# Completing each inverse to a whole token tile in the delta rule of a hybrid decoder layer

## The chip, the cores and the metric

The kernel runs on one core of a Trainium2 chip. The time is the device time of one launch in microseconds. Engines are named as the profile names them: PE (TensorE's products), PEld (its weight loads), DVE (VectorE), ACT (ScalarE), POOL (GpSimd), SP (SyncE, which issues most DMAs).

## The reference

One decoder layer on 256 tokens of width 2048: a normed input, one wide projection, two token mixers beside each other, gates, an output projection, a norm and a residual. All in float32. The change concerns the first mixer, the gated delta rule, of 8 heads of width 128, which is defined on chunks of 64 tokens:

```python
kb = k * beta[..., None]; vb = v * beta[..., None]
L = jnp.where(strict, jnp.einsum('bhnid,bhnjd->bhnij', kb, k) * decay, 0.0)
T = triangular_solve(L + eye, eye, left_side=True, lower=True)
u = jnp.einsum('bhnij,bhnje->bhnie', T, vb)
w = jnp.einsum('bhnij,bhnjd->bhnid', T, kb * jnp.exp(g)[..., None])
...
def step(state, inp):          # over the chunks
    v_new = u_i - jnp.einsum('bhcd,bhde->bhce', w_i, state)
    o = einsum(qg_i, state) + einsum(a_i, v_new)
    state = state * gl_i[..., None, None] + jnp.einsum('bhcd,bhce->bhde', kd_i, v_new)
```

With the decays carried along, this is one lower triangular system per head over the tokens: the new values of a stretch of tokens are its inverse triangle times (values less what earlier stretches contribute). It gives the same values whether it is cut in four stretches of 64 or in two of 128.

## The kernel before

Tokens lie in NT = 2 tiles of P = 128. The projections are the bulk of the work: `proj_t` and `proj_n` read weights in blocks of 1 MB over SP's queue, split each into a high and a low part (ACT and DVE, lines 225 and 226), and multiply in float32r. After every few products they call `tick()`. A tick counts half a unit, and lets the queues go on: each queue holds Python generators that issue some work and yield how many units to wait. So all the rest of the layer is issued between projection products, at places set by the yields: `SV_WAIT = 1` is two ticks, `L_WAIT = 5` is ten. PE takes its products in exactly the order in which they are issued (`mm` on line 147, `tr` on line 150, both pinned).

The delta rule is in the queue `gq`, in this order: `score_pair` for each pair of heads, `inverse`, `solve`.

`score_pair` writes `sl(h)`, the decayed products of keys and of queries, per head and token tile, and stores the four 64x64 triangles of each head to `l_d` in DRAM.

`inverse` inverts all 32 triangles (4 chunks, 8 heads) at once on DVE, 63 steps of two operations with `tv` and `tw`, issued at line 657 and 664. It stores the result to `t_d` (line 667) and loads it transposed into the tile `tt` (line 673), all on POOL's queue, and yields `L_WAIT`. `inv[0]` holds, for token tile t and head h, the transposed inverse of the first 64 tokens on partitions 0 to 63 (`lo_`) and that of the second 64 on partitions 64 to 127 (`hi_`).

`solve` waits until the values are there (`vq`), then goes through seven calls of `step(t, which)`, each followed by a yield of `SV_WAIT`. Every call makes 8 products (one per head) into two PSUM tiles named `sv`, and empties these into the values `gvt`:

- `which` 0: the first 64 tokens' inverse times their values (ACT copies, line 902)
- `which` 1: the triangle's lower left block times these, taken off the second 64 tokens' values (DVE, line 904)
- `which` 2: the second 64 tokens' inverse times their values (ACT, line 906)
- `which` 3, between the two token tiles: the first tile's contribution to the second, 128x128 (DVE, line 908)

Then `normed` makes the outputs (`so`), norms and gates them into `oz`, branch weights are fetched, and, after all attention heads have passed their transposes (`attended`), `turned_outputs` transposes the outputs (`ot`). The attention of the other mixer (`ms`, `pp`, `po`) runs in queues of its own between the same projections. PSUM has four `aux` banks for all this small work and four for the projections.

Of the kernel before, what the change touches and what calls it, by code (L numbers as in the profile page):

```python
# [8 lines left out]
F32 = mybir.dt.float32  # L9
# [3 lines left out]
ALU = mybir.AluOpType  # L13
AX = mybir.AxisListType

P = 128
# [16 lines left out]
SV_WAIT = 1  # L33
# [41 lines left out]
def hybrid_layer(  # L75
# [15 lines left out]
    nc = tc.nc  # L91
    B, S, D = x.shape
    NT = S // P
    KT = D // P
    H = a_log.shape[1]
# [17 lines left out]
    big = ctx.enter_context(tc.tile_pool(name="big", bufs=1))  # L113
# [10 lines left out]
    def acc_tile(name):  # L124
        return acc.tile([P, 512], F32, tag="acc", name=name)

    def aux_tile(name):
        return aux.tile([P, 512], F32, tag="aux", name=name)
# [17 lines left out]
    def mm(*args, **kwargs):  # L146
        return pin(nc.tensor.matmul(*args, **kwargs))  # L147

    def tr(*args):
        return pin(nc.tensor.transpose(*args))  # L150
# [26 lines left out]
    ident = cst.tile([P, P], F32, name="ident")  # L177
# [59 lines left out]
    def turn(c):  # L237

        pts = []
        for k in range(4 * c, 4 * c + 4):  # L240
            if k % 2 == 0:
                pt = aux_tile(f"hTp_{k}")
            pts.append((k, pt[:, k % 2 * S : (k % 2 + 1) * S]))
            for t in range(NT):
                tr(pts[-1][1][:, t * P : (t + 1) * P], xs[t][:, k * P : (k + 1) * P], ident)
        return pts
# [48 lines left out]
    pts = turn(0)  # L295
# [185 lines left out]
    gsl, gvt = [], []  # L481
# [5 lines left out]
    def sl(h):  # L487
        return gsl[h // HG][:, h % HG, :]

    def vt(t, h):  # L490
        return gvt[h // HG][:, t, h % HG, :]
# [9 lines left out]
    t_d = dram.tile([4, H, 64, 64], F32, name="t_d")  # L501
# [107 lines left out]
    def queries(p):  # L609
        h = 2 * p  # L610
        pq = proj_t(CQ + h * P, f"q{h}")
        qTs = [halves(pq[m], f"q{h + m}") for m in range(2)]
        for m in range(2):
            conv_silu(qTs[m], h + m)
        gq.add(score_pair(h, kTs[p], qTs))
        if p == H // 2 - 1:
            gq.add(inverse())
            gq.add(solve())


    inv = []

    def inverse():
        lc = big.tile([P, 64, 64], F32, tag="u1", name="lc")
        tv = big.tile([P, 16, 64], F32, tag="tv", name="tv")
        tw = big.tile([P, 16, 64], F32, tag="tw", name="tw")

        nc.gpsimd.memset(tv, 1.0)
        for g in range(4):
            nc.gpsimd.affine_select(  # L630
                out=tv[32 * g : 32 * g + 32],
                in_=tv[32 * g : 32 * g + 32],
                compare_op=ALU.is_equal,
                fill=0.0,
                base=g,
                pattern=[[4, 16], [-1, 64]],
                channel_multiplier=0,
            )

        rows = [slice(16 * r, 16 * r + 16) for r in range(4)]  # L640
        yield 0.5
        for js in rows:
            nc.gpsimd.dma_start(lc[0:32, js], l_d.rearrange("b h j i -> (b h) j i")[:, js])

        def copy(r, g):
            pin(nc.scalar.copy(lc[32 * g : 32 * g + 32, rows[r]], lc[0:32, rows[r]]))

        yield LC_WAIT
        for g in range(1, 4):
            copy(0, g)  # L650
            yield 0.5
        for j in range(63):
            if j < 48 and j % 16 in (4, 7, 10):
                copy(j // 16 + 1, (j % 16 - 1) // 3)
            n, r = j // 4 + 1, 63 - j
            pin(
                nc.vector.tensor_tensor(
                    tw[:, :n, :r],
                    lc[:, j : j + 1, j + 1 :].to_broadcast([P, n, r]),
                    tv[:, :n, j : j + 1].to_broadcast([P, n, r]),  # L660
                    op=ALU.mult,
                )
            )
            pin(nc.vector.tensor_tensor(tv[:, :n, j + 1 :], tv[:, :n, j + 1 :], tw[:, :n, :r], op=ALU.subtract))
            yield INV[after[0] > 0]
        for g in range(4):
            nc.gpsimd.dma_start(
                t_d.rearrange("b h (c g) i -> g (b h) c i", g=4)[g], tv[32 * g : 32 * g + 32]
            )
        inv.append(big.tile([P, NT, H, 64], F32, tag="tt", name="tt"))  # L670
        for p_ in range(2):
            for t in range(NT):
                nc.gpsimd.dma_start(
                    inv[0][p_ * 64 : p_ * 64 + 64, t, :, :], t_d[2 * t + p_].rearrange("h c i -> c h i")
                )
        yield L_WAIT


    def v_tok(h, vT):
        yield V_WAIT if h % 2 == 0 else 0.5  # L680
        while sc_left[0]:
            yield 1
        pv = aux_tile(f"vt_{h}")
        for t in range(NT):
            tr(pv[:, t * P : (t + 1) * P], vT[:, t * P : (t + 1) * P], ident)
        nc.vector.tensor_tensor(
            gvt[h // HG][:, :, h % HG, :],
            pv[:, : 2 * P].rearrange("p (t e) -> p t e", t=NT),
            sk[:, :, h : h + 1].to_broadcast([P, NT, P]),
            op=ALU.mult,  # L690
        )
# [182 lines left out]
    def solve():  # L874
        oT = big.tile([P, H, 2 * S], F32R, tag="u1", name="oaT")
        oaT[0] = oT
        lo_, hi_ = slice(0, 64), slice(64, 128)

        def step(t, which):
            for g in range(2):  # L880
                ps = aux_tile(f"sv_{t}_{which}_{g}")
                p3 = ps.rearrange("p (h e) -> p h e", e=P)
                for hh in range(4):
                    h = g * 4 + hh
                    o_ = slice(hh * P, (hh + 1) * P)
                    if which == 0:
                        mm(ps[lo_, o_], inv[0][lo_, t, h, :], vt(t, h)[lo_], start=True, stop=True)
                    elif which == 1:
                        mm(
                            ps[hi_, o_],  # L890
                            sl(h)[lo_, t * 4 * P + 64 : t * 4 * P + 128],
                            vt(t, h)[lo_],
                            start=True,
                            stop=True,
                        )
                    elif which == 2:
                        mm(ps[hi_, o_], inv[0][hi_, t, h, :], vt(t, h)[hi_], start=True, stop=True)
                    else:
                        mm(ps[:, o_], sl(h)[:, P : 2 * P], vt(0, h), start=True, stop=True)
                v_ = gvt[g][:, t]  # L900
                if which == 0:
                    nc.scalar.copy(v_[lo_], p3[lo_])
                elif which == 1:
                    nc.vector.tensor_tensor(v_[hi_], v_[hi_], p3[hi_], op=ALU.subtract)
                elif which == 2:
                    nc.scalar.copy(v_[hi_], p3[hi_])
                else:
                    nc.vector.tensor_tensor(gvt[g][:, 1], gvt[g][:, 1], p3, op=ALU.subtract)

# [83 lines left out]

        while vq.items or v_left[0]:
            yield 1
        for t in range(NT):
            for which in range(3):
                step(t, which)
                yield SV_WAIT
            if t == 0:  # L1000
                step(0, 3)
                yield SV_WAIT
        ozs = [big.tile([P, 2, HG, P], F32, tag=tg, name=f"oz_{t}") for t, tg in enumerate(("tv", "tw"))]
        for t in range(NT):
            yield from normed(t, ozs[t])
# [106 lines left out]
    for blk in ORDER:  # L1112
        n, c = blk[:2].rstrip("0123456789"), int(blk[-1])
# [123 lines left out]
    for tg, n in (("g0", 4), ("ga", 4), ("u1", 4)):  # L1237
        tl = big.tile([P, n, 2, 512], F32R, tag=tg, name=f"keep_{tg}")
# [22 lines left out]
    c = 3  # L1261
    pts = [acc_tile(f"a_y{c}_{t}") for t in range(NT)]
# [43 lines left out]
```

## Time and profile before

| | us |
|---|---|
| three runs | 778.04, 778.52, 779.99 |
| median | 778.52 |
| the profiled execution | 777.05 |
| its span in the trace | 775.4 |
| first and last product of the solve start (`sv`) | 365.1 and 397.6 |

The profile is of one execution. Its page gives the busy time of each engine, the chain of work that ended last, and the costliest groups of instructions; a row of a timeline gives the start and duration in us, then engine, line, operation, what is written and read, and shapes. Products of f32 by f32 appear as two records each, their f32 transposes as one. "[idle before <- releaser]" is how long the engine stood idle and what ended it. Records of PE overlap: the next one starts before the end of the one before, so distances between starts count.

### The profile page before, as it was taken

Reading aid. Unit: us, or ns where it says so; the run is one execution under the profiler, and the core shown is the slowest. Engines: PE = TensorE matmul, PEld = TensorE weight load, DVE = VectorE, ACT = ScalarE, POOL = GpSimd, SP = SyncE. Lnnn points to the kernel's source line nnn. Section 1 sums busy time; section 2 is a strip of 40 time slices with the busy share of each in tenths; the row PEclk is TensorE's granted clock in tenths of the full one; section 3 lists DMA queues with packets and bytes.
Section 4 is the critical chain, followed back from the end, with each engine's and each line's share of the span. In section 5 each row is a group of like instructions: output and inputs, shape, how many; then the busy total and the mean of one; then the engine's idle time right before and its main releaser. Section 6 shows DMA issues by size and latency. Waiting matters only on the chain.

```text
span 775.4 us, 10348 instructions
## 1 busy us (share of the span) xinstructions
PE 763.5 (98%) x3923; PEld 650.2 (84%) x3923; DVE 565.2 (73%) x914; ACT 436.1 (56%) x654; POOL 33.5 (4%) x61
## 2 busy tenths in 40 slices
PE   8999999999999999999999999999999999999995
PEld 7898988899888888888889888788888888888884
DVE  5777669885878898775547886686658776888853
ACT  5676666657655664454447475654455544556731
POOL 3000001112000000002001000000000000000000
PEclk9999999999999999999999999999999999999999
DMA  8576675457655556668336556657644956375912
GB/s 302 173 238 214 188 213 170 136 166 220 202 179 202 177 188 196 198 180 217 109 97 217 178 173 216 242 205 251 212 163 152 386 172 212 111 286 193 333 54 109
DMA packets 93656, 151.87 MB, mean 196 GB/s; under 512 B 3237, under 2 KB 46886, under 8 KB 93094
## 3 DMA queue, kind: packets, MB, share of 16 engines
q1 hardware_dynamic: 88902, 134.42, 53.4%
q0 software_dynamic: 4128, 15.74, 6.0%
q10 hardware_dynamic: 576, 1.05, 0.4%
q8 instruction: 31, 0.51, 0.3%
q14 instruction: 19, 0.16, 0.1%
HBM read 148.04 MB, written 3.15 MB: 195 GB/s over the span
## 4 chain that ended last, share of the span: by engine, by line
PE 95%; ACT 2%; DVE 2%; DMA 1%; SPq 0%; issue 0%; DVEq 0%
PE a_gb L147 11%; PE a_y L147 11%; PE a_ga L147 11%; PE a_zg L147 6%; PE a_mq L147 6%; PE a_v L147 6%; PE a_mk L147 6%; PE a_ub L147 6%; PE a_zm L147 6%; PE a_mv L147 5%; PE a_k L147 5%; PE a_ua L147 5%; PE a_q L147 4%; PE sv L147 2%; PE s L147 1%; DMA x<-in_x_dram 1%
## 5 line engine op out<-in xcount | busy, mean ns | idle before, releaser
L147 PE MATMUL a_ga<-hi_ga,hT 128*128 128x512 f32 x256 | 81.9, 393 | 0.0
L147 PE MATMUL a_gb<-hi_gb,hT 128*128 128x512 f32 x256 | 80.2, 390 | 0.0
L226 DVE TENSOR_TENSOR lo_gb<-raw_gb,hi_gb 128x1024 fp32r<-128x1024 f32 x32 | 38.9, 1223 | 25.1 <-ACT hi_gb L225 24.9
L147 PEld LDWEIGHTS a_gb<-hi_gb,hT 128*128 128x128 f32 x256 | 48.0, 188 | 10.6
L147 PEld LDWEIGHTS a_ga<-hi_ga,hT 128*128 128x128 f32 x256 | 48.1, 188 | 10.1
L225 ACT CAST hi_gb<-raw_gb 128x1024 fp32r<-128x1024 f32 x32 | 33.3, 1051 | 35.6 <-PE a_gb L147 26.5
L225 ACT CAST hi_ga<-raw_ga 128x1024 fp32r<-128x1024 f32 x32 | 33.7, 1055 | 34.0 <-PE a_ga L147 16.2
L226 DVE TENSOR_TENSOR lo_ga<-raw_ga,hi_ga 128x1024 fp32r<-128x1024 f32 x32 | 39.0, 1222 | 18.5 <-ACT hi_ga L225 18.3
L147 PE MATMUL a_ga<-lo_ga,hT 128*128 128x512 f32 x128 | 50.0, 391 | 0.1
L147 PE MATMUL a_gb<-lo_gb,hT 128*128 128x512 f32 x128 | 50.0, 391 | 0.0
L147 PE MATMUL a_zg<-hi_zg,hT 128*128 128x348 f32 (+1 forms) x192 | 47.0, 322 | 0.0
L147 PE MATMUL a_mq<-hT,hi_mq 128*128 128x512 f32 x128 | 46.8, 407 | 0.0
L147 PE MATMUL a_mk<-hT,hi_mk 128*128 128x512 f32 x128 | 46.1, 402 | 0.0
L147 PE MATMUL a_y<-hi_y,mT 128*128 128x512 f32 x144 | 46.1, 392 | 0.0
L147 PE MATMUL a_q<-hT,hi_q 128*128 128x512 f32 x128 | 46.0, 399 | 0.0
L147 PE MATMUL a_v<-hT,hi_v 128*128 128x512 f32 x128 | 45.3, 399 | 0.0
L147 PE MATMUL a_ub<-hi_ub,obT 128*128 128x512 f32 x128 | 41.3, 395 | 0.0
L147 PE MATMUL a_k<-hT,hi_k 128*128 128x512 f32 x128 | 40.6, 399 | 0.5 <-ACT hi_k L278 0.5
L147 PE MATMUL a_zm<-hi_zm,hT 128*128 128x512 f32 x128 | 40.5, 392 | 0.0
L147 PE MATMUL a_mv<-hi_mv,hT 128*128 128x512 f32 x128 | 40.1, 391 | 0.0
L147 PE MATMUL a_v<-hT,lo_v 128*128 128x256 f32 x128 | 35.9, 281 | 0.0
L147 PE MATMUL a_q<-hT,lo_q 128*128 128x256 f32 x128 | 35.9, 281 | 0.0
(377 smaller groups left out, 1972.8 us busy)
## 6 DMA issues: line engine op xcount, KB each, us to landing
raw_ga<-in_w_in_dram SPq DMA_DIRECT2D x16, 1024.0 KB, 5.1
raw_gb<-in_w_in_dram SPq DMA_DIRECT2D x16, 1024.0 KB, 5.7
raw_y<-in_w_out_dram SPq DMA_DIRECT2D x15, 1024.0 KB, 5.9
raw_q<-in_w_in_dram SPq DMA_DIRECT2D x8, 1024.0 KB, 5.6
raw_mv<-in_w_in_dram SPq DMA_DIRECT2D x8, 1024.0 KB, 5.1
raw_v<-in_w_in_dram SPq DMA_DIRECT2D x8, 1024.0 KB, 5.7
raw_zm<-in_w_in_dram SPq DMA_DIRECT2D x8, 1024.0 KB, 5.0
raw_mq<-in_w_in_dram SPq DMA_DIRECT2D x8, 1024.0 KB, 5.8
```

The costliest lines, as they stand in the source:

```text
L147: return pin(nc.tensor.matmul(*args, **kwargs))
L225: nc.scalar.copy(hi, raw)
L226: nc.vector.tensor_tensor(lo, raw, hi.bitcast(F32), op=ALU.subtract)
```

## The change

`inverse` no longer ends with the loads. The two token tiles get a tile each, `inv[t]` of 128 partitions x 8 heads x 128, in the tags `tt` and `tw`. POOL clears the quarter that stays zero and loads the two transposed 64x64 inverses onto the diagonal. After `L_WAIT` three groups of small products follow, each over both token tiles and all heads, each followed by `SV_WAIT`: `tl` transposes the first inverse back, `ltl` multiplies the lower left block of the triangle by it, `tlt` multiplies that by the second inverse; with its sign turned it is the fourth quarter. `tmp`, in the tag `tv`, holds the two results between. In `solve` each token tile then needs one step with its 128x128 inverse, and the step between the tiles stays: three calls of `step` in place of seven.

```diff
--- before.py
+++ after.py
@@ -667,14 +667,41 @@
             nc.gpsimd.dma_start(
                 t_d.rearrange("b h (c g) i -> g (b h) c i", g=4)[g], tv[32 * g : 32 * g + 32]
             )
-        inv.append(big.tile([P, NT, H, 64], F32, tag="tt", name="tt"))
-        for p_ in range(2):
-            for t in range(NT):
-                nc.gpsimd.dma_start(
-                    inv[0][p_ * 64 : p_ * 64 + 64, t, :, :], t_d[2 * t + p_].rearrange("h c i -> c h i")
-                )
+
+        for t, tag in enumerate(("tt", "tw")):
+            tl = big.tile([P, H, P], F32, tag=tag, name=f"inv_{t}")
+            inv.append(tl)
+            nc.gpsimd.memset(tl[64:P, :, 0:64], 0.0)
+            for p_ in range(2):
+                ps = slice(p_ * 64, p_ * 64 + 64)
+                nc.gpsimd.dma_start(tl[ps, :, ps], t_d[2 * t + p_].rearrange("h c i -> c h i"))
         yield L_WAIT
 
+        lo_, hi_ = slice(0, 64), slice(64, 128)
+        tmp = big.tile([P, NT, H, 64], F32, tag="tv", name="tmp")
+
+        def blocks(name):
+            pts = [aux_tile(f"{name}_{t}") for t in range(NT)]
+            return [pt.rearrange("p (h c) -> p h c", h=H) for pt in pts]
+
+        pb = blocks("tl")
+        for t in range(NT):
+            for h in range(H):
+                tr(pb[t][lo_, h, :], inv[t][lo_, h, 0:64], ident[lo_, lo_])
+            nc.scalar.copy(tmp[lo_, t], pb[t][lo_])
+        yield SV_WAIT
+        pb = blocks("ltl")
+        for t in range(NT):
+            for h in range(H):
+                mm(pb[t][hi_, h, :], sl(h)[lo_, t * 4 * P + 64 : t * 4 * P + 128], tmp[lo_, t, h], start=True, stop=True)
+            nc.scalar.copy(tmp[hi_, t], pb[t][hi_])
+        yield SV_WAIT
+        pb = blocks("tlt")
+        for t in range(NT):
+            for h in range(H):
+                mm(pb[t][lo_, h, :], tmp[hi_, t, h], inv[t][hi_, h, 64:128], start=True, stop=True)
+            nc.vector.tensor_scalar_mul(inv[t][lo_, :, 64:128], pb[t][lo_], -1.0)
+        yield SV_WAIT
 
     def v_tok(h, vT):
         yield V_WAIT if h % 2 == 0 else 0.5
@@ -874,8 +901,6 @@
     def solve():
         oT = big.tile([P, H, 2 * S], F32R, tag="u1", name="oaT")
         oaT[0] = oT
-        lo_, hi_ = slice(0, 64), slice(64, 128)
-
         def step(t, which):
             for g in range(2):
                 ps = aux_tile(f"sv_{t}_{which}_{g}")
@@ -883,27 +908,10 @@
                 for hh in range(4):
                     h = g * 4 + hh
                     o_ = slice(hh * P, (hh + 1) * P)
-                    if which == 0:
-                        mm(ps[lo_, o_], inv[0][lo_, t, h, :], vt(t, h)[lo_], start=True, stop=True)
-                    elif which == 1:
-                        mm(
-                            ps[hi_, o_],
-                            sl(h)[lo_, t * 4 * P + 64 : t * 4 * P + 128],
-                            vt(t, h)[lo_],
-                            start=True,
-                            stop=True,
-                        )
-                    elif which == 2:
-                        mm(ps[hi_, o_], inv[0][hi_, t, h, :], vt(t, h)[hi_], start=True, stop=True)
-                    else:
-                        mm(ps[:, o_], sl(h)[:, P : 2 * P], vt(0, h), start=True, stop=True)
-                v_ = gvt[g][:, t]
+                    w = inv[t][:, h, :] if which == 0 else sl(h)[:, P : 2 * P]
+                    mm(ps[:, o_], w, vt(0 if which else t, h), start=True, stop=True)
                 if which == 0:
-                    nc.scalar.copy(v_[lo_], p3[lo_])
-                elif which == 1:
-                    nc.vector.tensor_tensor(v_[hi_], v_[hi_], p3[hi_], op=ALU.subtract)
-                elif which == 2:
-                    nc.scalar.copy(v_[hi_], p3[hi_])
+                    nc.scalar.copy(gvt[g][:, t], p3)
                 else:
                     nc.vector.tensor_tensor(gvt[g][:, 1], gvt[g][:, 1], p3, op=ALU.subtract)
 
@@ -993,13 +1001,9 @@
 
         while vq.items or v_left[0]:
             yield 1
-        for t in range(NT):
-            for which in range(3):
-                step(t, which)
-                yield SV_WAIT
-            if t == 0:
-                step(0, 3)
-                yield SV_WAIT
+        for t, which in ((0, 0), (0, 1), (1, 0)):
+            step(t, which)
+            yield SV_WAIT
         ozs = [big.tile([P, 2, HG, P], F32, tag=tg, name=f"oz_{t}") for t, tg in enumerate(("tv", "tw"))]
         for t in range(NT):
             yield from normed(t, ozs[t])
```

## The prediction

> **What bounds the kernel now.** I read the page first: the busy times and the chain that ended last.
>
> ```profile
> span 775.4 us, 10348 instructions
> ...
> PE 763.5 (98%) x3923; PEld 650.2 (84%) x3923; DVE 565.2 (73%) x914; ACT 436.1 (56%) x654; POOL 33.5 (4%) x61
> ...
> PE 95%; ACT 2%; DVE 2%; DMA 1%; SPq 0%; issue 0%; DVEq 0%
> ```
>
> TensorE (PE) is in 95% of the chain. The waits of PE alone confirm it: these four are all it has.
>
> ```profile
> PE hTp L150 <- DMA x<-in_x_dram: 1.5, 2, 0.9
> PE warm L147 <- DVE epst L181: 1.1, 1, 1.1
> PE ms L147 <- DVE y_mk L1084: 0.7, 1, 0.7
> PE a_k L147 <- ACT hi_k L278: 0.5, 1, 0.5
> ```
>
> None of them stands in the solve. So a product taken out of PE's stream shortens the kernel by the time it held the stream, and one put in lengthens it. Work on ACT, DVE and POOL counts only where PE comes to wait for it. Next I asked for the instructions that write or read `sv`, the PSUM tiles of the solve.
>
> ```profile
> L147 PEld LDWEIGHTS sv<-gdn,tt x64: 129/133/133, 365.1 to 397.5; 64*64 64x64 f32 x64
> L147 PE MATMUL sv<-gdn,tt x64: 269/269/320, 365.1 to 397.6; 64*64 64x128 f32 x64
> L147 PEld LDWEIGHTS sv<-gdn x48: 129/133/192, 369.9 to 392.6; 64*64 64x64 f32 x32, 128*128 128x128 f32 x16
> L902 ACT COPY gdn<-sv x4: 579/580/581, 366.2 to 387.5; 64x512 f32<-64x512 f32 x4
> L904 DVE TENSOR_TENSOR gdn<-gdn,sv x4: 691/691/691, 371.1 to 393.1; 64x512 f32<-64x512 f32 x4
> L906 ACT COPY gdn<-sv x4: 581/581/581, 377.6 to 397.9; 64x512 f32<-64x512 f32 x4
> L908 DVE TENSOR_TENSOR gdn<-gdn,sv x2: 680/683/686, 382.2 to 382.9; 128x512 f32<-128x512 f32 x2
> ```
>
> A product of f32 by f32 is two records: the 32 products with the inverse (two half-steps, two token tiles, eight heads) are the x64 of the first row. In all there are 112 records in seven groups of 16: six groups of 64x64 and one of 128x128. A duration in these rows (269 ns) is not what a record holds the stream for, since matmuls are pipelined. For that I read starts in the timeline of PE, around the first 64x64 group and around the 128x128 one.
>
> ```profile
> 364.88 0.28 PE L147 MATMUL a_mq<-hT,lo_mq 128*128 128x256 f32 x1
> 365.09 1.96 PE L147 MATMUL sv<-gdn,tt 64*64 64x128 f32 x16
> 366.98 0.50 PE L147 MATMUL a_mq<-hT,hi_mq 128*128 128x512 f32 x1
> 367.32 0.28 PE L147 MATMUL a_mq<-hT,lo_mq 128*128 128x256 f32 x1
> 367.44 0.39 PE L147 MATMUL a_mq<-hT,hi_mq 128*128 128x512 f32 x1
> 367.67 0.27 PE L147 MATMUL a_mq<-hT,lo_mq 128*128 128x256 f32 x1
> ...
> 380.78 0.27 PE L147 MATMUL a_mq<-hT,lo_mq 128*128 128x256 f32 x1
> 380.89 1.95 PE L147 MATMUL sv<-gdn 128*128 128x128 f32 x16
> 382.60 0.47 PE L147 MATMUL a_mq<-hT,hi_mq 128*128 128x512 f32 x1
> 382.91 0.28 PE L147 MATMUL a_mq<-hT,lo_mq 128*128 128x256 f32 x1
> ```
>
> Undisturbed, a 256-column record is followed after 0.12 us (367.32 to 367.44) and a 512-column one after 0.23 us (367.44 to 367.67): the time goes with the columns. So after the record at 364.88 the next 256-column one was due at 364.88+0.12+0.23 = 365.23; it came at 367.32. **A 64x64 group costs 2.09 us.** The same sum at 380.78 gives 381.13 against 382.91: **the 128x128 group costs 1.78 us.** Its 16 records start 1.71 us apart from what follows (380.89 to 382.60), 0.107 us each. Taking the same for the 64x64 group, 2.09-1.71 = 0.38 us of it lie around the records: it starts 0.21 instead of 0.12 us after its predecessor, and the products behind it start late. The solve as it stands: 6x2.09+1.78 = **14.32 us**. (Three groups are followed by attention products, which share a little of the 0.38; I leave that in on both sides.)
>
> **The change, part by part: PE.** Six 64x64 groups and one of 128x128 go. In come, each between two yields: `tl`, 16 transposes of 64x64; `ltl`, 16 products of 64x64 on 64 columns; `tlt`, 16 more; then three groups of 8 products of 128x128, at the price of the present one. A transpose is one record, as the three of each of two heads show:
>
> ```profile
> 387.44 0.88 PE L150 MATMUL pp<-ident,s 128*128 128x128 f32 x6
> 388.07 0.47 PE L147 MATMUL a_mk<-hT,hi_mk 128*128 128x512 f32 x1
> ```
>
> Six of them hold 0.63 us, 0.105 each. So `tl` is 16 records, `ltl` and `tlt` 32 each: 80 records whose moving side has 64 columns. No stream of such records is in the trace. From below: time goes with the columns, half of 0.107 is 0.053 us. From above: no gain from the narrower side, 0.107, or 0.113 at the pace of the rows above ((1.96-0.27)/15). Loading the weights might set a floor between: 64 columns take 133 ns and 128 take 192 in the rows of `sv`, some 0.06 us for the 64 more. I take 0.06, near the lower end, since in the present 64x64 group the load does not show beside the product: with weights of half the width its records are as far apart as those of the 128x128 group.
>
> - `tl`: 16x0.06+0.38 = 1.34
> - `ltl` and `tlt`: 2x(32x0.06+0.38) = 4.60
> - three 128x128 groups: 3x1.78 = 5.34
>
> That is 11.28 us in place of 14.32: **-3.0 us**. With 0.053 us a record it is -3.6; with 0.113 it is 80x0.113+1.14+5.34 = 15.52, +1.2.
>
> The Trainium skill ("TensorE: Matmul & The Clock Gate", Part 3, The mechanism) says that a weight load overlaps matmuls in flight only when it goes to another row group. All products of one of these groups are in the same row group, so by that rule load and product follow each other, at 0.06+0.053 = 0.113 us a record, which is the +1.2. The trace speaks against it: by the same rule the 64x64 group of before would take 16x(0.06+0.107) = 2.7 us for its records and not the 1.89 from 365.09 to 366.98.
>
> **ACT and DVE.** The eight half-width ACT copies (0.58 us each) become four half-width ones (`tl`, `ltl`) and four of full width; an operation's time goes with its 512 columns and not with its partitions, as L904 (64) and L908 (128) show with 0.69 and 0.68. Eight copies as before. DVE loses four subtracts of 0.69 and gets two scaled evacuations of the same width. None of this holds PE unless it is late for the next group.
>
> ```profile
> 367.08 0.58 ACT L902 COPY gdn<-sv 64x512 f32<-64x512 f32 x1 [0.29 <-PE sv L147]
> ...
> 374.73 1.05 ACT L225 CAST hi_mk<-raw_mk 128x1024 fp32r<-128x1024 f32 x1 [5.12 <-DVE s L1040]
> ```
>
> The second copy of the first step is done at 367.66, and the second group starts at 369.95 (in the timeline of `sv` it is the first of the x48, "369.9"): 2.3 us in hand. The new hand-offs (`tl` to `ltl`, `ltl` to `tlt`, `tlt` to the solve) have the same two ticks of projection work between them, one `SV_WAIT`, so I cost them at nothing. Behind a group that waits, all projections stand, since PE takes its work in order. The second row shows the danger: ACT is in order too and stood idle for 5.12 us in front of a weight cast.
>
> **POOL and its DMAs.** Still four stores to `t_d` and four loads of 128 KB. Two memsets (64 partitions x 512) are new in POOL's queue, the second ahead of the last two loads, and the loads land as eight pieces of 256 B per partition instead of one run.
>
> ```profile
> L673 POOL DMA_DIRECT2D tt<-t_d x4: 682/690/711, 354.0 to 356.0; - x4
> DMA to landing us min/median/max: 4.4/4.6/6.6
> ```
> ```profile
> 2.70 0.94 POOL L628 MEMSET tv<- 128x1024 f32 x1
> ```
>
> The last load is issued at 356.0 and landed by 362.6; half of 0.94, 0.5 us, is a memset. So 363.1, and the first group needs its data at 365.09: 2 us in hand. Before, the first group needed one quarter of the loads; `tl` needs three of four. The next work behind on POOL's queue is the fetch of branch weights some 50 us later; SP's queue, with the projections' weights, is not passed.
>
> **The order.** Seven yields of the solve become six, so the output products start two ticks, some 5 us, sooner in the stream. Nobody takes them sooner:
>
> ```profile
> 449.99 0.81 PE L150 MATMUL pp<-ident,s 128*128 128x128 f32 x6
> ...
> 452.47 1.03 PE L150 MATMUL ot<-ident,oz 128*128 128x128 f32 x8
> ```
>
> The transposes of the outputs follow the last attention heads' `pp`, on which `attended` waits. I put no gain on it.
>
> **The sum.** The profiled execution took 777.05 us (span 775.4 and 1.65 around it); 777.05-3.04 = 774.0. It lies 1.47 below the median of the runs, 778.52, so the median becomes **775.5 us**. A measurement of this kernel can tell about 0.3%, 2.3 us, from no change: the three runs of before lie within 1.95 us.
>
> **Rivals.** *First, slower than before: narrow products are no cheaper.* A fixed price per load and product keeps the 80 new records at the pace of the wide ones. It decides above (14.32-1.14-5.34)/80 = 0.098 us a record and ends at +1.2, 779.7. For it: nothing in the trace runs faster than 0.105 us a record. Against it: 256 and 512 columns scale as they should, and the weight load is hidden.
>
> *Second: the inverse lands late.* If pieces of 256 B double the landing time, the last load is there at 356.5+13.2 = 369.7, `tl` holds PE for up to 4.6 us, and the sum is +1.6, 780.1. It turns to a loss where the wait passes 3.0 us, a landing behind 368.1. Against it: the far end of these loads, in DRAM, is already in pieces of 256 B, and they landed in 4.6 us in the median.
>
> *Third: a hand-off is late.* If the copy of `tl` or `ltl` comes to stand behind a cast like that of 374.73, PE waits about 5.12+1.05-2.3 = 3.9 us: +0.9 for one, +4.8 for two (783.3). Against it: that cast waited for the projection products on PE that stand behind the group, so a copy put behind it would not fit the program's order; and the copies of the present steps, in the same place, were never waited for.
>
> **How the numbers follow.** Forecast 0.58: of this 0.50 beyond 2.3 us (up to about 0.068 us a record), 0.08 within. First rival 0.16: 0.11 within 0.3%, 0.05 slower with any stall of 1.1 us on top. Second 0.12: 0.07 within, 0.05 slower. Third 0.14: 0.06 within, 0.08 slower. Faster 0.50, same 0.32, slower 0.18. The range goes from the lowest run with the best pace, 778.04-3.6 = 774.4, to the first rival's 779.7; beyond it lie the worse halves of the second and third. The forecast alone: 774.4 to 776.9.
>
> **What would show it.** Right: `tl` in 1.3 us of PE's stream, `ltl` and `tlt` in 2.3 each, 128x128 groups in 1.8, no wait of PE between the first transposes and the last `sv`, the transposes of the outputs still behind the last `pp`. Wrong: records of 64 columns 0.1 us apart (first rival), a wait in front of `tl` for the loads (second), or waits of `ltl` or `tlt` for ACT (third).

## The result: 5 us faster, a microsecond below the range

| | before | changed |
|---|---|---|
| runs beside each other, median | 778.52 (777.05 to 779.99, 5) | 773.40 (772.77 to 774.99, 5) |
| ratio, 95% interval | | 0.9939 (0.992 to 0.9958) |
| profiled execution, span | 775.4 | 773.2 |

Two later comparisons of the same two kernels gave 0.9946 (0.9934 to 0.9958) and 0.9941 (0.9928 to 0.9954): 3.3 to 5.6 us by their intervals; the first one's interval is 3.3 to 6.2 us. The forecast was 3.0 us faster, and 775.5 in a range from 774.4.

The page and the waits of PE in the changed kernel:

```profile
span 773.2 us, 10375 instructions
...
PE 96%; ACT 2%; DVE 1%; DMA 1%; issue 0%; SPq 0%; DVEq 0%
```
```profile
PE hTp L150 <- DMA x<-in_x_dram: 1.3, 2, 0.7
PE warm L147 <- DVE epst L181: 1.1, 1, 1.1
```

PE is the bound as before. Of its four waits the two in the first microseconds are left here; that of `a_k` comes and goes from run to run, and that of `ms` is gone. The new groups in the timeline of PE:

```profile
366.72 0.28 PE L147 MATMUL a_mq<-hT,lo_mq 128*128 128x256 f32 x1
366.93 1.08 PE L150 MATMUL tl<-ident,inv 64*64 64x64 f32 x16
367.94 0.50 PE L147 MATMUL a_mq<-hT,hi_mq 128*128 128x512 f32 x1
368.28 0.28 PE L147 MATMUL a_mq<-hT,lo_mq 128*128 128x256 f32 x1
...
377.09 0.28 PE L147 MATMUL a_mq<-hT,lo_mq 128*128 128x256 f32 x1
377.30 2.08 PE L147 MATMUL tlt<-inv,tmp 64*64 64x64 f32 x32
379.30 0.50 PE L147 MATMUL a_mq<-hT,hi_mq 128*128 128x512 f32 x1
379.64 0.28 PE L147 MATMUL a_mq<-hT,lo_mq 128*128 128x256 f32 x1
```

By the sum of the prediction (0.35 us from one 256-column record to the next), `tl` costs 368.28-367.07 = 1.21 us and `tlt` 379.64-377.44 = 2.20. The pace within a group needs the duration of one record, from the rows of the tile `tlt`:

```profile
L147 PE MATMUL tlt<-inv,tmp x32: 218/218/267, 377.3 to 379.2; 64*64 64x64 f32 x32
```

(2.08-0.218)/31 = 0.060 us from one record to the next.

To see where the time went, I compared the starts of the same projection blocks in both timelines: of `a_mq` ahead of the solve, of `a_mq` behind it, and of the first `a_ua`. Before:

```profile
363.61 0.39 PE L147 MATMUL a_mq<-hT,hi_mq 128*128 128x512 f32 x1
...
405.12 0.48 PE L147 MATMUL a_mq<-hT,hi_mq 128*128 128x512 f32 x1
...
485.92 0.48 PE L147 MATMUL a_ua<-hi_ua0p,oaT 128*128 128x512 f32 x1
```

After:

```profile
365.45 0.39 PE L147 MATMUL a_mq<-hT,hi_mq 128*128 128x512 f32 x1
...
403.92 0.40 PE L147 MATMUL a_mq<-hT,hi_mq 128*128 128x512 f32 x1
...
483.76 0.48 PE L147 MATMUL a_ua<-hi_ua0p,oaT 128*128 128x512 f32 x1
```

| stretch, us | before | after | difference |
|---|---|---|---|
| start to `a_mq` ahead of the solve | 363.61 | 365.45 | +1.84 |
| to `a_mq` behind the solve | 41.51 | 38.47 | **-3.04** |
| to the first `a_ua` | 80.80 | 79.84 | **-0.96** |
| to the end | 289.5 | 289.5 | 0.0 |

So the solve gave what was forecast, another microsecond came behind it, and this one execution lost 1.84 us before the stretch of the change had begun. The split is good to about 0.1 us: before, the block at 405.12 stands right behind output products (`so`), after, the one at 403.92 does not. The experiments are on the last two.

The -0.96 stands at the attention's products `ms`. In the timeline of DVE and of PE before:

```profile
437.93 1.21 DVE L747 TENSOR_TENSOR tq_g<-tq_g 128x1024 f32<-128x1024 f32 x1
439.07 0.41 DVE L462 TENSOR_TENSOR y_mk<-a_mk,y_mk 128x256 f32<-128x256 f32 x1
439.40 1.21 DVE L747 TENSOR_TENSOR tq_z<-tq_z,tq_g 128x1024 f32<-128x1024 f32 x1
440.53 0.42 DVE L1084 TENSOR_TENSOR y_mk<-y_mk,rrow 128x256 f32<-128x256 f32 x1
```
```profile
439.28 0.39 PE L147 MATMUL a_ga<-hi_ga,hT 128*128 128x512 f32 x1
439.51 0.82 PE L147 MATMUL ms<-y_mk,y_mq 128*128 128x128 f32 x4
441.00 0.92 PE L147 MATMUL ms<-y_mk,y_mq 128*128 128x128 f32 x4 [0.68 <-DVE y_mk L1084]
441.57 0.59 PE L147 MATMUL a_ga<-hi_ga,hT 128*128 128x512 f32 x1
```

The last keys, `y_mk`, stood behind two differences of branch weights (L747, pinned in DVE's order), and PE waited for them. After, the same differences (now L774) come sooner, and the keys are ready ahead of `ms`, which runs in one piece:

```profile
433.83 1.22 DVE L774 TENSOR_TENSOR tq_g<-tq_g 128x1024 f32<-128x1024 f32 x1
434.97 0.42 DVE L462 TENSOR_TENSOR y_mk<-a_mk,y_mk 128x256 f32<-128x256 f32 x1
435.30 1.22 DVE L774 TENSOR_TENSOR tq_z<-tq_z,tq_g 128x1024 f32<-128x1024 f32 x1
436.43 0.42 DVE L462 TENSOR_TENSOR y_mk<-a_mk,y_mk 128x256 f32<-128x256 f32 x1
436.77 0.75 DVE L1088 TENSOR_TENSOR y_mk<-y_mk,rrow 128x256 f32<-128x256 f32 x2
```
```profile
438.04 0.39 PE L147 MATMUL a_ga<-hi_ga,hT 128*128 128x512 f32 x1
438.27 1.47 PE L147 MATMUL ms<-y_mk,y_mq 128*128 128x128 f32 x8
439.39 0.58 PE L147 MATMUL a_ga<-hi_ga,hT 128*128 128x512 f32 x1
```

From the last projection record ahead of these `ms` to the first behind them it is 441.57-439.28 = 2.29 us before and 439.39-438.04 = 1.35 after: 0.94 of the 0.96 us lies here.

### The profile page after: what moved, and what is told of

It reads as the page before. It is cut to its first block, busy times and chain, and to the rows that moved or that the text cites. A ratio compares the mean times of both kernels' runs of the same rounds, so it can differ in the third digit from the quotient of the medians.

```text
span 773.2 us, 10375 instructions
## 1 busy us (share of the span) xinstructions
PE 762.8 (99%) x3939; PEld 651.2 (84%) x3939; DVE 563.5 (73%) x912; ACT 433.7 (56%) x652; POOL 34.6 (4%) x63
## 4 chain that ended last, share of the span: by engine, by line
PE 96%; ACT 2%; DVE 1%; DMA 1%; issue 0%; SPq 0%; DVEq 0%
PE a_gb L147 11%; PE a_ga L147 11%; PE a_y L147 11%; PE a_k L147 6%; PE a_zg L147 6%; PE a_mq L147 6%; PE a_v L147 6%; PE a_mk L147 6%; PE a_ub L147 6%; PE a_zm L147 6%; PE a_mv L147 5%; PE a_ua L147 5%; PE a_q L147 4%; PE s L147 1%; PE ms L147 1%; PE po L147 1%
## 5 line engine op out<-in xcount | busy, mean ns | idle before, releaser
L147 PE MATMUL a_ga<-hi_ga,hT 128*128 128x512 f32 x256 | 82.1, 394 | 0.0
L147 PE MATMUL a_gb<-hi_gb,hT 128*128 128x512 f32 x256 | 80.1, 390 | 0.0
L147 PEld LDWEIGHTS a_gb<-hi_gb,hT 128*128 128x128 f32 x256 | 48.0, 188 | 10.5
L147 PEld LDWEIGHTS a_ga<-hi_ga,hT 128*128 128x128 f32 x256 | 48.1, 188 | 10.0
L147 PE MATMUL a_ga<-lo_ga,hT 128*128 128x512 f32 x128 | 50.1, 391 | 0.1
L147 PE MATMUL a_gb<-lo_gb,hT 128*128 128x512 f32 x128 | 50.1, 391 | 0.0
L147 PE MATMUL a_zg<-hi_zg,hT 128*128 128x348 f32 (+1 forms) x192 | 47.1, 322 | 0.0
L147 PE MATMUL a_mq<-hT,hi_mq 128*128 128x512 f32 x128 | 47.0, 407 | 0.0
L147 PE MATMUL a_mk<-hT,hi_mk 128*128 128x512 f32 x128 | 46.2, 402 | 0.0
L147 PE MATMUL a_y<-hi_y,mT 128*128 128x512 f32 x144 | 46.0, 392 | 0.0
L147 PE MATMUL a_q<-hT,hi_q 128*128 128x512 f32 x128 | 46.0, 399 | 0.0
L147 PE MATMUL a_v<-hT,hi_v 128*128 128x512 f32 x128 | 45.3, 399 | 0.0
L147 PE MATMUL a_k<-hT,hi_k 128*128 128x512 f32 x128 | 41.8, 410 | 0.0
L147 PE MATMUL a_ub<-hi_ub,obT 128*128 128x512 f32 x128 | 41.3, 395 | 0.0
L147 PE MATMUL a_zm<-hi_zm,hT 128*128 128x512 f32 x128 | 40.5, 392 | 0.0
L147 PE MATMUL a_mv<-hi_mv,hT 128*128 128x512 f32 x128 | 40.1, 390 | 0.0
L147 PE MATMUL a_v<-hT,lo_v 128*128 128x256 f32 x128 | 35.9, 281 | 0.0
L147 PE MATMUL a_q<-hT,lo_q 128*128 128x256 f32 x128 | 35.9, 281 | 0.0
```

## The experiments

"In the trace" below is the same comparison of blocks; "by the times" are ratios to the kernel before.

**The changed kernel again, and a third time.**

> The changed kernel once more, as it is, for a second trace and more times. Theory A (stream and order): 3.05 us come from TensorE's stream in the solve and 0.95 us from a wait of the attention's products for VectorE that is gone; 4.0 us in all, so about 774.5 us where the kernel before takes 778.5; the first products at half pace, which put the trace of the changed kernel 1.75 us behind in its first 12 us, are of that execution and not of the kernel, and need not come again. Rival B (the whole 5.1 us belong to the change): about 773.4, and the start is as slow as in the first trace.

774.22 us (773.83 to 774.72), by the ratio of 0.9946 4.2 us below before. In the trace -3.05 and -0.95. PE reached the projection block `a_zg` at 35.85 us, against 34.82 in the trace of before and 36.57 in the first one of the changed kernel; in the third trace of the changed kernel it did so at 34.89. This is Theory A: the start is not the kernel's. In the fourteen traces of this study, of all its kernels, that block began between 34.8 and 36.7. In the timelines the start shows as the pace of the first products; before and changed:

```profile
8.23 1.17 PE L147 MATMUL a_k<-hT,hi_k 128*128 128x512 f32 x4 [0.46 <-ACT hi_k L278]
```
```profile
8.75 2.05 PE L147 MATMUL a_k<-hT,hi_k 128*128 128x512 f32 x4
```

The same four records take 1.17 us or 2.05: little more than half the pace. With it the block `a_zg` moves by up to 1.8 us. The Trainium skill ("TensorE: Matmul & The Clock Gate", Part 1, What's actually happening) says that the clock is raised by a free-running window of about 3.4 us, so that how many products run slow varies from run to run. The traces agree in part: in that of the kernel with the transposes on DVE, below, these four records took 2.05 us too, and its granted clock is 0.50 from 8 to 10 us; in the first trace of the changed kernel the granted clock is given as 1.00 there, so that the clock was down in that one is likely by the pace, and not shown.

**The outputs back at their old ticks.** In the changed kernel:

```diff
         for t, which in ((0, 0), (0, 1), (1, 0)):
             step(t, which)
             yield SV_WAIT
+        yield SV_WAIT
```

> The changed kernel with one more yield of SV_WAIT between the solve and the output products, so that these, the fetch of the branch weights and their differences are issued at the ticks of the kernel before. Theory A: the wait of the attention's last products for VectorE comes back, 0.7 to 1.0 us; 0.95 us slower than the changed kernel, some 3 us faster than before. Rival B (the order has nothing to do with it; VectorE is free because the solve gives it less to do): the wait stays away, same time as the changed kernel.

774.32 us (0.9947). By the times the 0.95 us does not show: the median is 0.1 above the 774.22 of the changed kernel, with a scatter of 1.7 us. The trace shows it: +0.95 in the stretch behind the solve, with the wait there again and 2.29 us around `ms`; the solve itself differs by 0.13, and the rest lies ahead of it. The row of the wait, from the waits of PE:

```profile
PE ms L147 <- DVE y_mk L1089: 0.7, 1, 0.7
```

**The order alone, without the change.** In the kernel before, once by a constant and once by a yield:

```diff
-T_WAIT = (5, 7, 7)
+T_WAIT = (6, 7, 7)
```

> The kernel before with one constant changed: the first entry of T_WAIT from 5 to 6, so that the first weight differences are issued two ticks later. The delta rule is as before. Theory A: the differences no longer stand ahead of the last attention pair's keys on VectorE, the wait of the attention's products goes, and the kernel is 0.7 to 1.0 us faster than before without any change of the solve. Rival B: no change within 0.3 us; or the differences come later and stand ahead of something else, then slower by up to 1 us.

```diff
                 step(t, which)
-                yield SV_WAIT
+                if (t, which) != (1, 2):
+                    yield SV_WAIT
```

> The kernel before without the last yield of the solve, so that its output products, the fetch and the differences are issued two ticks sooner, as in the changed kernel; the seven steps stay. Theory A: the attention's wait goes, 0.95 us faster than before from that; against it the output products now follow the last step at once and a PSUM bank may not be free yet, up to 0.7 us. Between 0.2 and 1.0 us faster. Rival B: no faster than before.

The first: 776.33 us, 0.9974 (0.9966 to 0.9983), in the trace -0.99 in the stretch behind the solve. The second: 777.10, 0.9985 (0.9977 to 0.9994), -0.99. Neither trace has a wait of `ms`; around `ms` they show 1.34 and 1.35 us, as the changed kernel does. So the order alone gives about a microsecond. Two ticks sooner, the differences still stand ahead of the last keys, but DVE is done with the keys at 439.74 and `ms` starts at 440.49; two ticks later, one difference stands among the operations of the last keys (at 438.71) where there were two. By its times the first gained 1.3 to 2.6 us, more than its trace shows; what the rest is stays open.

**What the groups cost.** The three groups left out of the changed kernel, and issued twice:

```diff
+            nc.gpsimd.memset(tl[0:64, :, 64:128], 0.0)
...
-        pb = blocks("tl")
...
+        for _ in range(3):
+            yield SV_WAIT
```

> The changed kernel without the three groups of small products and their evacuations (the fourth quarter of each inverse is cleared instead; the yields stay). It leaves out that part of the solve. Theory A (the groups hold TensorE's stream, and nothing else does): 1.2 for the transposes and 2.2 each for the two groups of products, together 5.6 us less than the changed kernel, taken at the three places in the stream. Rival C (the groups partly fill gaps): less than 4 us.

```diff
-                tr(pb[t][lo_, h, :], inv[t][lo_, h, 0:64], ident[lo_, lo_])
+                for _ in range(2):
+                    tr(pb[t][lo_, h, :], inv[t][lo_, h, 0:64], ident[lo_, lo_])
...
```

> The changed kernel with each of the 16 transposes and 32 products of the three groups issued twice in a row, to the same place: 80 more records of 64 columns, no more changes of the array's shape. Theory A: 80 x 0.06 = 4.8 us slower than the changed kernel, all in the three groups; what the groups cost beyond that in the kernel without them (5.6 - 4.8 = 0.8, some 0.27 a group) is the price of stopping the stream. Rival C (narrow records cost little, the stop is the price): under 3 us.

Without: 768.12 us, -5.62 in the trace, all of it in the stretch of the solve; the starts in the stream gave 1.21+2x2.20 = 5.61. Twice: 778.71, +4.61 in the trace, 0.058 us for each of 80 records. So the groups fill no gaps: what they take is what the kernel loses. The rest, 5.62-4.61 = 1.01 or 0.34 a group, is the price of stopping the stream (forecast 0.38). First rival of the prediction: refuted.

**The transposes on DVE.** To find a faster version, the 16 transposes were moved off PE:

```diff
-                tr(pb[t][lo_, h, :], inv[t][lo_, h, 0:64], ident[lo_, lo_])
-            nc.scalar.copy(tmp[lo_, t], pb[t][lo_])
...
+            for src, rows_, c0 in ((qa, qa, 0), (qa, qb, 32), (qb, qb, 32)):
...
+                nc.vector.transpose(tmp[rows_, t, :, f0 : f0 + 32], inv[t][src, :, c0 : c0 + 32])
```

> The changed kernel with the first inverses turned back on VectorE, in blocks of 32x32, in place of the 16 transposes on TensorE and their copies. Theory A: TensorE's stream loses the 1.2 us of the transposes, VectorE's six operations lie in its idle time: 1.2 us faster than the changed kernel, some 5.2 faster than before. If VectorE is late for the next group, TensorE waits there and the gain is gone.

776.71 us, and 2.04 us slower than the changed kernel in the trace where 1.2 faster was hoped. It is the third rival of the prediction come true, a late hand-off: PE waited for DVE, whose last blocks stood behind a weight part. And behind the wait the clock fell. Rows of the table by stretches (the columns are PE, PEld, DVE, ACT, POOL busy, the granted clock, DMA share and GB/s):

```profile
370.00:372.00 2.00, 0.89 (x15) 0.92 (x16) 0.93 (x3) 0.39 (x1) 0.00 (x0) 1.00 0.52 111
372.00:374.00 2.00, 2.00 (x11) 1.71 (x10) 0.56 (x2) 0.58 (x1) 0.00 (x0) 0.65 1.04 338
374.00:376.00 2.00, 2.00 (x7) 1.67 (x6) 1.98 (x8) 0.99 (x4) 0.00 (x0) 0.50 0.25 83
```
```profile
371.11 1.11 PE L147 MATMUL ltl<-tmp,gdn 64*64 64x64 f32 x16 [1.38 <-DVE tmp L692]
```

A wait of 1.38 us, and in the 4 us behind it a granted clock of 0.65 and then 0.50. The eleven traces without a wait in the solve have 1.00 in all of it. Of the twelve executions three took 773.4 to 773.5, with a mean granted clock of 0.998, and nine 775.7 to 777.5, with 0.992 to 0.996: where the clock held, the kernel was over 2 us faster.

**Pairs in different rows of the array.** The second token tile takes its two products in opposite order, so that neighbours use different halves of the rows:

```diff
+        for h in range(H):
+            mm(pb[0][hi_, h, :], sl(h)[lo_, 64:128], tmp[lo_, 0, h], start=True, stop=True)
+            mm(pb[1][lo_, h, :], tmp[hi_, 1, h], inv[1][hi_, h, 64:128], start=True, stop=True)
...
+        for h in range(H):
+            mm(pb[0][lo_, h, :], tmp[hi_, 0, h], inv[0][hi_, h, 64:128], start=True, stop=True)
+            mm(pb[1][lo_, h, :], tmp[lo_, 1, h], inv[1][lo_, h, 64:128], start=True, stop=True)
```

> As the one before, and the two token tiles take their two products in opposite order (the second tile's lower left block is turned on VectorE too, eight small operations), so that neighbouring products sit in different halves of the array's rows. If products in different halves run beside each other, the 32 records of a group take about half their 1.9 us: 1 to 2 us faster than with the turning alone. If they follow each other as now: the same time, and each group keeps its 0.06 us a record.

774.75 us: still a wait for DVE of 2.1 us and the half clock behind it (0.73 and 0.50 in the stretches from 370 to 374), but 1.34 us less in the solve than the one before: the 32 records of `tlt` took 1.15 us in place of 2.07.

Two ways to keep the pairs and lose the wait. First, the turning two ticks sooner:

```diff
-        yield L_WAIT
+        yield L_WAIT - 1
...
-        yield SV_WAIT
+        yield SV_WAIT + 1
```

> As the kernel with pairs, with the turning on VectorE issued two ticks sooner (L_WAIT less 1) and the first products at the same tick (one unit more behind it). If the late hand-off and the half clock behind it were all that the two VectorE kernels lost, TensorE now waits for nothing: against the changed kernel the transposes go (1.2 us) and the two groups take 1.1 instead of 2.0 us each, 3.0 us in all; about 771.2 where the changed kernel takes 774.2. If VectorE is held up by the loads of the inverse instead and its weight parts come late, TensorE waits for those and the gain is under 1 us.

774.34 us (771.99 to 775.09). The wait is there still, 1.8 us: DVE turned the eight blocks of the lower left part first, from 365.09, then did keys and a weight part, and came to the blocks of the inverses at 370.13. In this trace the clock stayed at 1.00 behind the wait, and the solve was 1.13 us shorter than in the changed kernel. The times show that only in part: the execution of 771.99 had a mean clock of 0.997, the five from 773.8 to 775.1 had 0.994 to 0.996. Second, all turning on PE:

```diff
                 tr(pb[t][lo_, h, :], inv[t][lo_, h, 0:64], ident[lo_, lo_])
+                if t == 1:
+                    mm(pb[t][hi_, h, :], sl(h)[lo_, 4 * P + 64 : 4 * P + 128], ident[lo_, lo_], start=True, stop=True)
```

> The changed kernel with the two token tiles' products in pairs in different halves of the array's rows, and all turning on TensorE: the second tile's lower left block is turned there too, as 8 products with the identity (16 records more in the first group, about 0.9 us). The two groups of products lose 0.9 us each. Together 0.9 us faster than the changed kernel, 773.3 to 773.6; no wait of TensorE.

775.22 us, 0.97 us slower in the trace. No wait, and the pairs are quick, but transposes and products by turns hold each other up:

```profile
366.10 0.33 PE L147 MATMUL tl<-ident,gdn 64*64 64x64 f32 x2
366.36 0.24 PE L150 MATMUL tl<-ident,inv 64*64 64x64 f32 x1
366.53 0.33 PE L147 MATMUL tl<-ident,gdn 64*64 64x64 f32 x2
```

Three records take 0.43 us, where 0.18 was counted. The two kinds of record also write different halves of PSUM's partitions, and no run separates the change of kind from the change of half, so which of them costs the time is open.

**The best of both.** The changed kernel's own transposes, the pairs, and on DVE only the second tile's lower left block, which is in place long before; DVE is done with it 2 us ahead of `ltl`:

> The changed kernel with its own transposes of the first inverses on TensorE, and the two groups of products in pairs in different halves of the array's rows; only the second tile's lower left block is turned on VectorE, long before it is needed. No wait of TensorE; the two groups take 1.1 instead of 2.0 us each, 1.9 us faster than the changed kernel (772.3 where that takes 774.2), 0.7% faster than before with the rest. If VectorE's eight operations make TensorE wait as in the kernels before, the gain is lost.

> The changed kernel beside the one with pairs on the same chip: 4.0 us faster than before, 1.9 us slower than the one with pairs.

772.22 us (771.04 to 773.18), 0.9919 (0.9905 to 0.9934) of before; the changed kernel beside it 773.81 (772.73 to 774.82), 0.9941. In the trace the solve is 1.84 us shorter than in the changed kernel, and PE has only its waits of the first microseconds. `tlt`:

```profile
375.62 1.15 PE L147 MATMUL tlt<-inv,tmp 64*64 64x64 f32 x32
376.69 0.50 PE L147 MATMUL a_mq<-hT,hi_mq 128*128 128x512 f32 x1
```

This version beats both.

## Why the prediction missed

Its main term was right: 3.04 us forecast in the solve, 3.04, 3.05 and 3.04 in the three traces of the changed kernel. That it fits to the second decimal is luck. By parts: 0.06 us a record (measured 0.060), `tl` 1.34 (1.21), `tlt` 2.30 (2.20), 128x128 groups 1.78 (384.20-382.42 = 1.78, from the rows below). With `ltl` at the 2.20 of `tlt` the groups go from 14.32 to 10.95, 3.37 less. Three small differences take 0.33 of that back: attention products cost 0.1 us more behind the new groups than behind the old; the 56 undisturbed pairs of projection records between the groups follow each other after 0.350 us in place of 0.348, 0.14 together; and the rest is the mark behind `so`.

```profile
382.07 0.28 PE L147 MATMUL a_mq<-hT,lo_mq 128*128 128x256 f32 x1
382.19 1.95 PE L147 MATMUL sv<-gdn,inv 128*128 128x128 f32 x16
383.89 0.48 PE L147 MATMUL a_mq<-hT,hi_mq 128*128 128x512 f32 x1
384.20 0.28 PE L147 MATMUL a_mq<-hT,lo_mq 128*128 128x256 f32 x1
```

The rule that the prediction took from the Trainium skill ("TensorE: Matmul & The Clock Gate", Part 3, The mechanism), that a load overlaps only with products in other row groups, was rightly set aside: it is 0.060 us a record within one row group, and not 0.113.

The step that failed is **The order**: "Nobody takes them sooner", and no gain put on it. That held for the outputs' transposes, but the end of the solve also sets when the branch weights' differences are issued, and these sat on DVE in front of the keys that PE waited for. The wait was quoted in the first part, "PE ms L147 <- DVE y_mk L1084", and put aside because it does not stand in the solve. Its worth is 0.96 us, the idle 0.68 and what lies around it, and the two kernels that shift only the order gained it without the change. With it the sum would have been 4.0, which lies within the intervals of all three comparisons (by their ratios 4.7, 4.2 and 4.6).

The range failed with it. Its low end was one lowest run of three less the best pace; later runs of the kernel before went down to 776.6, and the start alone moves an execution by up to 1.8 us. With the wait in it the sum gives 774.5, inside the range, and the first median, 773.40, is still 1.1 lower. That rest is not put down to a step: the two later medians of the changed kernel are 774.22 and 773.81, and a range for one measurement has to hold such scatter as well.

Second rival (the loads): it did not come true. In the first trace of the changed kernel the loads landed in 7.6 us in the median and 7.9 at most in place of 4.6 and 6.6, and the last was there 2.0 us ahead of `tl`. In its other two traces they landed in 4.9 and 5.0 (5.3 at most), so the 7.6 is no price of the smaller pieces. The memsets cost these loads nothing: one ran at 174.0, the other at 351.7, while POOL waited for the stores.

```profile
L677 POOL DMA_DIRECT2D inv<-t_d x4: 684/690/716, 354.9 to 357.0; - x4
...
DMA to landing us min/median/max: 6.8/7.6/7.9
```

Third rival (a hand-off): not in the changed kernel, but in all three kernels that turn the inverses on DVE, and it can be dearer than the wait itself: with the transposes on DVE the 1.21 us of `tl` were saved and the solve was still 2.04 longer, 3.25 in all for a wait of 1.38.

## What to carry to other kernels

Where one engine bounds a kernel, cost an edit by what it takes from that engine's stream, from start to start around a group: here this was right to 0.1 us. Then follow what the edit moves in the queues, not only what takes its result: each wait that the bounding engine still has, wherever it stands, is asked which work it stood behind, and whether the edit shifts that. And compare two traces block by block before believing a median: a difference ahead of the change is not the change's.

## What the hardware showed

- Products of 64x64 in different halves of the array's rows run beside each other: 32 records in 1.15 us against 2.08, about 0.030 us each in place of 0.060. The Trainium skill ("TensorE: Matmul & The Clock Gate", Part 3, The mechanism) says that tiles in other row groups overlap; here it holds for f32.
- Behind waits of PE of 1.4 and 2.1 us the granted clock fell to 0.50 within the next 4 us; behind one of 1.8 us it stayed at 1.00. The Trainium skill ("TensorE: Matmul & The Clock Gate", Part 1, HAM oscillation) puts the idle time that this takes at over about 3.4 us; these waits were shorter.
- Alternating transposes and products of 64x64, which here write different halves of PSUM's partitions, cost about 0.25 us for each pair of changes (0.43 us a turn in place of 0.18), where either alone runs at 0.06 us a record.
